# Weight sums at half the pace, one seventh raw buffer, and a quarter of the residual rows scaled earlier: a two-layer fp32 decoder trunk on one core

## The chip, the cores and the metric

One Trainium2 chip, one core in use. The metric is the device time of one execution in microseconds; the times shown are medians over several executions. Engines are named as the profile names them: PE (TensorE matmul), PEld (its weight load), DVE (VectorE), ACT (ScalarE), POOL (GpSimd), SP (SyncE, which here only issues DMAs). Lnnn is line nnn of the kernel before.

## The reference

Two layers, 512 tokens, width 2048, all in fp32. Per layer:

```python
h = einsum('bsd,dn->bsn', x, w_in)             # one projection, split into three head groups
y_fox = fox_attention(q, k, v, cum_logf)       # 6 heads, causal, with a forget bias
y_dsa = dsa_attention(rope(q), rope(k), v, q_idx, k_idx, w_idx)   # 6 heads, top 128 keys by an indexer
y_mem = memory_attention(q, k_mem, v_mem)      # 4 heads over 256 memory tokens
y = concat([y_g * silu(gate_g) for the three groups])
x = layer_norm(ALPHA * x + y @ w_out, ln_gain, ln_bias)
```

## The kernel before

**Matrix products.** TensorE is used in the format fp32r. Each fp32 operand is split into a high and a low part (`split`: ACT copies the high part, L218, DVE subtracts it, L219), and a product is three matmuls (L225 to L227). The weights come in chunks of 128 x 2048 from one long tensor `wall`. A chunk is two halves of 128 x 1024. SP loads a half into one of six `raw` buffers (L259); its split goes to one of four pairs `whi`/`wlo`; PE then uses it.

**Order of the work.** The main loop walks over the chunks in a list written out by hand, and PE runs in that order. Per layer: `mv`, `mk` (memory keys and values, 8 chunks), `small`, `iq` (indexer, 8), `vs` (values, gates and part of the queries, 70), heads (16 chunks `fq`, `fk`, `dq`, `dk`) and `out` (28). While chunk i runs, chunk i+2 is loaded (`load_w`) and the half 1.5 chunks ahead is split. Everything else is a generator that is advanced by `tick`, once in the middle and once at the end of a chunk; a generator that yields k rests for k ticks. Those begun with `whole=True` get no tick in the middle of a `vs` or `out` chunk. The value of `now[1]` names the stage: kv, index, values, heads, out.

**Strassen form.** `vs` and `out` are computed by Winograd's variant of Strassen's product: seven products over five pairs of column blocks (`vs`), each with two chunks (g = 0, 1). The 70 `vs` chunks are numbered here from 0: pair p takes 10p to 10p+9 in the order P1 P1 P7 P7 P2 Q6 Q6 P2 Q4 Q4, then come four chunks for each pair, 50+4p to 53+4p, in the order Q5 Q5 Q3 Q3. The right-hand sides are sums of weight blocks, made in four ways:

- T3 (for P7), and T1 (for Q5) of the pairs below `IN_DRAM`, are made in DRAM by POOL's DMAs, 1 MB each: a copy (L427), then an accumulating DMA (L407). `value_sums` yields after each, `paced` says how many ticks pass to the next, and `load_w` later loads the sum (`raw<-sum`). Outside the stage "values" each such DMA is also held back until DVE has come to a mark (`pool_waits`, L397 and L398).
- T1 of the other pairs is made on chip: SP loads the second block in four pieces into `slots` (`other`, L265) and DVE adds it to the raw halves (`pair_w`, L276).
- Q6 grows out of P7: POOL accumulates one more block from DRAM into the raw half (`grow_w`, L284).
- Q4 comes out of Q6 and P2: DVE adds the two raw halves (`make_w`, L294). Until then P7's four halves and two of P2's are all held.

**Buffers.** Everything else lives in one pool of 71 `slots` of 128 x 512; a new tile takes the slot that was set free longest ago, and its first instruction waits until that slot is really free. DMAs wait in the same way at the head of their queue: SP and POOL each issue strictly in order. Results of `vs` are stored to DRAM (`store_v`, L977 and L979) and loaded again head by head (`load_head`, L986). `attend` handles one head, `mem_head` one memory head (`MEM_TURNS` says after which chunks heads 1 to 3 begin).

**Between the layers.** `next_x` normalises the residual `z`, turns it (PE), applies gain and bias by column on ACT (L1053) for the next projection, makes the low parts on DVE and POOL (L1057), and stores the bare normalised `z` to `x1_d` (L1040). `residual_rows`, in the `vs` stage of layer 1 from chunk 6 on, loads these 16 tiles again (L1087), applies gain and bias by row (L1077, L1078; the rows come from `load_row`, L1027) and stores them (L1079) for the residual of layer 1.

Of the kernel before, what the change touches and what calls it, by code (L numbers as in the profile page):

```python
# [14 lines left out]
ALU = mybir.AluOpType  # L15
# [32 lines left out]
HEADS = (("f", 0), ("f", 4), ("f", 5), ("f", 1), ("d", 0), ("d", 1), ("f", 2), ("d", 2), ("d", 3),  # L48
         ("f", 3), ("d", 4), ("d", 5))
EARLY = 4  # L50
MEM_TURNS = [("fq", 4), ("fk", 4), ("fk", 5)]
HEAD_CHUNKS = ([(c, h) for h in range(EARLY, H_FOX) for c in ("fq", "fk")]
               + [(c, h) for h in range(H_DSA) for c in ("dq", "dk")])

# [27 lines left out]
             ("Q5", 0), ("Q5", 1), ("P2", 0), ("Q3", 0), ("P2", 1), ("Q3", 1))  # L82
PAIRS = 5
MEMQ, FOXQ, VALUES, GATES = 0, 2, 4, 7
IN_DRAM = 2
VAL_FIRST = (("P1", 0), ("P1", 1), ("P7", 0), ("P7", 1), ("P2", 0), ("Q6", 0), ("Q6", 1), ("P2", 1),
             ("Q4", 0), ("Q4", 1))
VAL_SECOND = (("Q5", 0), ("Q5", 1), ("Q3", 0), ("Q3", 1))
# [89 lines left out]
def kernel(  # L178
# [12 lines left out]
):  # L191
    nc = tc.nc
    consts = ctx.enter_context(tc.tile_pool(name="consts", bufs=1))
    raws = ctx.enter_context(tc.tile_pool(name="raws", bufs=6))
    whl = ctx.enter_context(tc.tile_pool(name="whl", bufs=4))
    slots = ctx.enter_context(tc.tile_pool(name="slots", bufs=71))
    tiny = ctx.enter_context(tc.tile_pool(name="tiny", bufs=3))
    psum = ctx.enter_context(tc.tile_pool(name="psum", bufs=8, space=bass.MemoryType.PSUM))
    dram = ctx.enter_context(tc.tile_pool(name="dram", bufs=1, space=bass.MemoryType.DRAM))
# [227 lines left out]
                            nc.gpsimd.dma_start(sums[key], src)  # L427
                        yield

    def paced(gen, steps=2):  # L430

        n = 0
        for _ in gen:
            n += 1
            while now[1] == "kv":
                yield 1
            yield {"heads": 1, "out": 3, "index": 2}.get(now[1], steps)

    def value_sums(l):

# [24 lines left out]
    now = (0, "index")  # L465
# [267 lines left out]
    def attend(l, kind, h):  # L733
        key = (kind, h)
        if kind == "f":
            bt = pr = biases.pop(h)
        q, k = qs.pop(key), ks.pop(key)
        ps = [bank("s") for _ in range(3)]
        for qb in (3, 1, 0, 2):
            b, off, w = PACK[qb]  # L740
            product(ps[b][:, off:off + w], tuple(a[:, qb * P:(qb + 1) * P] for a in q),
                    tuple(a[:, :w] for a in k), True, True)
        if kind == "d":
            assert l in chosen
            bt = masks[l]
            pr = [slot("pr", w=w) for w in BANK_W]
        nm, sums, rec = small("nm", 4), small("sums", 4), small("rec", 4)

        for qb in (3, 1, 0, 2):
            b, off, w = PACK[qb]  # L750
            c = slice(off, off + w)
            nc.vector.tensor_tensor_reduce(pr[b][:, c], ps[b][:, c], bt[b][:, c], -SCALE, -TAKEN,
                                           ALU.add, ALU.min, nm[:, qb:qb + 1])
        for qb in (3, 1, 0, 2):
            b, off, w = PACK[qb]
            nc.scalar.activation(pr[b][:, off:off + w], pr[b][:, off:off + w], AF.Exp,
                                 bias=nm[:, qb:qb + 1], scale=-1.0, accum_out=sums[:, qb:qb + 1])

        def probabilities():
            nc.vector.reciprocal(rec, sums)  # L760
            for qb in (3, 1, 0, 2):
                b, off, w = PACK[qb]
                nc.scalar.activation(pr[b][:, off:off + w], pr[b][:, off:off + w], AF.Copy,
                                     scale=rec[:, qb:qb + 1])

        before.append(probabilities)
        n = HEADS.index(key)
        load_head(("g", key), GATES + n // 4, n % 4)
        load_head(("v", key), VALUES + n // 4, n % 4)
        yield 2  # L770
        tp = [bank("pt") for _ in range(3)]
        for kt in range(4):
            tb, toff = PT_PACK[kt]
            for qb in range(kt, 4):
                b, off, w = PACK[qb]
                nc.tensor.transpose(tp[tb][:, toff + (qb - kt) * P:toff + (qb - kt + 1) * P],  # L776
                                    pr[b][:, off + kt * P:off + (kt + 1) * P], ident)
        pt = []
        for b in range(3):
            w = PT_W[b]  # L780
            if w == 512:
                hi, lo = slot("pth", F32R), slot("ptl", F32R)
            else:
                both = slot("pthl", F32R)
                hi, lo = both[:, :w], both[:, w:]
            split(tp[b][:, :w], hi, lo)
            pt.append((hi, lo))
        yield 1
        gate(key, turned(("g", key), "gt"))
        v = slot("vh", F32R), slot("vl", F32R)  # L790
        split(vraw.pop(("v", key)), *v)
        yield 1
        po = bank("po")
        for kt in range(4):
            tb, toff = PT_PACK[kt]
            w = SEQ - kt * P
            product(po[:, kt * P:], tuple(a[:, kt * P:(kt + 1) * P] for a in v),
                    tuple(a[:, toff:toff + w] for a in pt[tb]), kt == 0, kt == 3)
        heads_out(head_number(key), key, po)
# [182 lines left out]
    def load_head(key, j, c):  # L982

        assert all(stored[j, st] == 1 + j % 2 for st in range(4))
        t = vraw[key] = slot("vraw")
        nc.sync.dma_start(t.rearrange("p (s c) -> p s c", s=4),  # L986
                          v_d[j].rearrange("(s p) c -> p s c", s=4)[:, :, c * HD:(c + 1) * HD])
# [20 lines left out]
    z, stats = {}, {}  # L1008
# [13 lines left out]
    rows = {}  # L1022

    def load_row(l, c, eng):
        for name, src in (("g", gain), ("b", bias)):
            t = rows[name, c] = slot("row")
            eng.dma_start(t, bass.AP(tensor=src.tensor, offset=src.offset + l * DM + c * 512,  # L1027
                                     ap=[[0, P], [1, 512]]))
# [8 lines left out]
    def next_x():  # L1037

        def store(st, c):
            nc.gpsimd.dma_start(x1_d[st * P:(st + 1) * P, c * 512:(c + 1) * 512], z.pop((st, c)))  # L1040

        ms = [norm_stats(st) for st in range(4)]
        for c in range(4):
            for st in range(4):
                normalise(st, c, *ms[st])
            yield 1
        for k in range(KT):
            c, o = divmod(k, 4)
            tp = bank("xt")
            for st in range(4):  # L1050
                nc.tensor.transpose(tp[:, st * P:(st + 1) * P], z[st, c][:, o * P:(o + 1) * P], ident)
            xf, hi, lo = slot("xf"), slot("xh", F32R), slot("xl", F32R)
            nc.scalar.activation(xf, tp, AF.Identity, bias=gcol[:, 1, k:k + 1],  # L1053
                                 scale=gcol[:, 0, k:k + 1])
            nc.scalar.activation(hi, xf, AF.Copy)
            eng = nc.gpsimd if k % 2 else nc.vector
            eng.tensor_tensor(lo, xf, hi.bitcast(F32), op=ALU.subtract)  # L1057
            xT[k] = (hi, lo)
            first_sum(k, xf)
            if k % 2:  # L1060
                for st in (o - 1, o) if c else ():
                    store(st, c - 1)
                yield 1
        for st in range(4):
            store(st, 3)
            if st % 2:
                yield 1

    def residual_rows(l):

        tiles = [(st, c) for c in range(4) for st in range(4)]
        t = {}
        for n in range(len(tiles) + 1):
            if n:
                st, c = tiles[n - 1]
                d = t.pop(n - 1)
                nc.vector.tensor_tensor(d, d, rows["g", c], op=ALU.mult)  # L1077
                nc.vector.tensor_tensor(d, d, rows["b", c], op=ALU.add)  # L1078
                nc.gpsimd.dma_start(x1_d[st * P:(st + 1) * P, c * 512:(c + 1) * 512], d)  # L1079
                if st == 3:  # L1080
                    del rows["g", c], rows["b", c]
            if n < len(tiles):
                st, c = tiles[n]
                if st == 0:
                    load_row(l - 1, c, nc.sync)
                t[n] = slot("z")
                nc.sync.dma_start(t[n], x1_d[st * P:(st + 1) * P, c * 512:(c + 1) * 512])  # L1087
            yield 2

    terms = {}  # L1090

# [68 lines left out]
    for i, (kind, l, j, col, _) in enumerate(chunks):  # L1160
        late = last_half(i)
        if kind == "out":
            step = OUT_ORDER.index(j)
            name, pair = j
# [11 lines left out]
        elif kind == "vs":  # L1176
            name, pair = j
# [11 lines left out]
        for h in range(2):  # L1189
            n = 2 * i + h  # L1190
# [15 lines left out]
            if kind == "out" and late:  # L1206
# [6 lines left out]
                if len(kept) == 16:  # L1213
# [3 lines left out]
                    for c in (0, 256):  # L1217
                        ps = bank("z")
                        c = slice(c, c + 256)
# [17 lines left out]
            elif kind == "mv":  # L1237
                for m in range(2):
                    for nn in range(2):
                        k = 4 * col + 2 * h + nn  # L1240
                        c = (k % 2) * 256 + m * P
# [3 lines left out]
            elif kind == "mk":  # L1245
                for kk in range(8):
                    k = 8 * h + kk
                    m = memT[k // 2]
                    c = (k % 2) * 256
                    product(ps[:, :256], weight_cols(n, kk), tuple(a[:, c:c + 256] for a in m),  # L1250
                            k == 0, k == KT - 1)
            else:
                cols = slice(P if kind == "iq" else 0, SEQ)
                for kk in range(8):
                    k = 8 * h + kk
# [9 lines left out]
        if kind == "mk":  # L1265
            t = slot("kmem", F32R)
# [14 lines left out]
        elif kind in ("dq", "dk"):  # L1281
            t = rope(ps, cos_d, sin_d, HALVES, P, "rope")
# [8 lines left out]
        elif kind == "small":  # L1291
# [4 lines left out]
            t = index_rope(ps, 64, 0, nc.vector)  # L1296
            kh2, kl2 = slot("kh2", F32R), slot("kl2", F32R)
            for r in (0, 64):
                nc.scalar.activation(kh2[r:r + 64], t[:64], AF.Copy)
                nc.vector.tensor_tensor(kl2[r:r + 64], t[:64], kh2.bitcast(F32)[:64],  # L1300
                                        op=ALU.subtract)
            idx["k"] = (kh2, kl2)
            begin(small_work(l, sm))
        elif kind == "iq":
            t = index_rope(ps, P, P, nc.gpsimd)
# [12 lines left out]
        if kind == "mv" and l > 0:  # L1318
            now = (l, "kv")
        if kind == "small":  # L1320
            now = (l, "index")
# [140 lines left out]
```

## Time and profile before

| | |
|---|---|
| median of 3 runs | 1934.21 us (1932.75 to 1935.8) |
| the profiled execution | 1935.36 us, span 1933.6 us |
| granted TensorE clock | 0.994 |
| PE busy | 1898.5 us, 98% of the span |
| DVE, ACT, POOL busy | 1469.4, 1016.7, 372.9 us |
| DMA moved | 503.55 MB, mean 260 GB/s |

The profile is read in this way: PE is busy nearly always, so what can be won without changing the arithmetic are the stretches in which it waits or runs at a lower clock. Matmul durations overlap one another, so the count of matmuls in a stretch says more than the busy time.

### The profile page before, as it was taken

What the parts mean: (1) busy time and instruction counts of PE and PEld (TensorE: products, weight loads), DVE (VectorE), ACT (ScalarE), POOL (GpSimd) and SP (SyncE); (2) the same over time, 40 slices, a digit from 0 to 9 for tenths busy, and PEclk for the clock granted to TensorE, in tenths of its full rate; (3) what the DMA queues carried; (4) which work ended last, traced back from release to release, by engine and by line L of the source; (5) the groups of instructions that cost most, each with busy time, mean ns of one, the idle gap of its engine ahead of it and who ended that gap; (6) DMA issues with size and microseconds to landing.
All of it is one profiled execution on the core that took longest, in us unless ns stands there. A gap on an engine that the chain in (4) does not pass through costs nothing.

```text
span 1933.6 us, 26367 instructions
## 1 busy us (share of the span) xinstructions
PE 1898.5 (98%) x9250; PEld 1612.4 (83%) x9250; DVE 1469.4 (76%) x2374; ACT 1016.7 (53%) x1598; POOL 372.9 (19%) x610
## 2 busy tenths in 40 slices
PE   9999999999999999999999999999999999999997
PEld 8998777888888888888899987778888888888886
DVE  6888667887755677688877886799877566677888
ACT  5676334355456555554476753444544465555453
POOL 0122221221222012110061221221113120112101
PEclk9999999999999999999999999999999999999999
DMA  9777988999988788999886799987899786889966
GB/s 353 260 204 205 292 251 287 252 271 279 343 262 223 222 263 237 259 331 293 262 269 225 202 244 312 273 281 236 236 287 352 254 240 193 265 241 260 348 198 152
DMA packets 169906, 503.55 MB, mean 260 GB/s; under 512 B 17120, under 2 KB 62176, under 8 KB 160876
## 3 DMA queue, kind: packets, MB, share of 16 engines
q1 hardware_dynamic: 132876, 296.28, 44.5%
q0 software_dynamic: 36896, 205.57, 41.4%
q8 instruction: 73, 1.20, 0.2%
q14 instruction: 61, 0.50, 0.1%
HBM read 453.53 MB, written 176.19 MB: 326 GB/s over the span
## 4 chain that ended last, share of the span: by engine, by line
PE 70%; DMA 11%; DVE 11%; ACT 4%; issue 2%; POOL 1%; SPq 0%; DVEq 0%; ACTq 0%; POOLq 0%
DMA raw<-in_wall_dram 10%; PE v L226 8%; PE v L227 8%; PE v L225 8%; PE c L227 8%; PE c L225 8%; PE c L226 8%; DVE wlo L219 4%; PE z L226 4%; PE z L227 4%; PE z L225 4%; ACT whi L218 2%; PE pt L776 1%; DVE raw L294 1%; PE ix L693 1%
## 5 line engine op out<-in xcount | busy, mean ns | idle before, releaser
L219 DVE TENSOR_TENSOR wlo<-raw,whi 128x1024 fp32r<-128x1024 f32 (+1 forms) x521 | 634.7, 1224 | 273.6 <-ACT whi L218 270.2
L218 ACT ACTIVATE whi<-raw 128x1024 fp32r<-128x1024 f32 (+1 forms) x521 | 547.1, 1054 | 457.3 <-PE v L227 179.3
L225 PE MATMUL c<-xh,whi 128*128 128x512 f32 (+1 forms) x800 | 301.3, 377 | 0.0
L227 PE MATMUL c<-xh,wlo 128*128 128x512 f32 (+1 forms) x800 | 298.4, 373 | 0.0
L226 PE MATMUL c<-xl,whi 128*128 128x512 f32 (+1 forms) x800 | 297.8, 372 | 0.0
L226 PE MATMUL v<-wlo,vxh 128*128 128x512 f32 x640 | 249.5, 390 | 2.4 <-DVE wlo L219 2.4
L225 PE MATMUL v<-whi,vxh 128*128 128x512 f32 x640 | 249.7, 390 | 0.2 <-ACT whi L218 0.2
L227 PE MATMUL v<-whi,vxl 128*128 128x512 f32 x640 | 249.1, 389 | 0.0
L226 PE MATMUL v<-wlo,xh 128*128 128x512 f32 x480 | 190.2, 396 | 8.4 <-DVE wlo L219 8.4
L225 PE MATMUL v<-whi,xh 128*128 128x512 f32 x480 | 189.6, 395 | 6.0 <-ACT whi L218 5.9
L227 PE MATMUL v<-whi,xl 128*128 128x512 f32 x480 | 189.1, 394 | 0.0
L226 PE MATMUL z<-wlo,yh 128*128 128x512 f32 (+1 forms) x434 | 168.1, 387 | 2.5 <-DVE wlo L219 2.5
L225 PE MATMUL z<-whi,yh 128*128 128x512 f32 (+1 forms) x434 | 168.4, 388 | 0.0
L227 PEld LDWEIGHTS c<-xh,wlo 128*128 128x128 f32 x800 | 150.1, 188 | 21.9
L227 PE MATMUL z<-whi,yl 128*128 128x512 f32 (+1 forms) x434 | 167.8, 387 | 0.0
L226 PEld LDWEIGHTS c<-xl,whi 128*128 128x128 f32 x800 | 150.4, 188 | 20.7
L225 PEld LDWEIGHTS c<-xh,whi 128*128 128x128 f32 x800 | 150.3, 188 | 20.3
L226 PEld LDWEIGHTS v<-wlo,vxh 128*128 128x128 f32 x640 | 120.1, 188 | 28.6 <-DVE wlo L219 3.8
L398 POOL TENSOR_TENSOR seen<-mark,mhalf 128x1 f32<-128x1 f32 x91 | 23.6, 259 | 620.3 <-DVE mark L397 611.6
L225 PEld LDWEIGHTS v<-whi,vxh 128*128 128x128 f32 x640 | 120.1, 188 | 25.6 <-ACT whi L218 0.9
L227 PEld LDWEIGHTS v<-whi,vxl 128*128 128x128 f32 x640 | 120.1, 188 | 25.1
L226 PEld LDWEIGHTS v<-wlo,xh 128*128 128x128 f32 x480 | 91.3, 190 | 31.9 <-DVE wlo L219 12.9
(227 smaller groups left out, 3215.7 us busy)
## 6 DMA issues: line engine op xcount, KB each, us to landing
raw<-in_wall_dram SPq DMA_DIRECT2D x322, 512.0 KB, 7.4
sum<-in_wall_dram POOLq DMA_DIRECT2D x60, 1024.0 KB, 11.6
raw<-sum SPq DMA_DIRECT2D x120, 512.0 KB, 7.6
v<-vraw POOLq DMA_DIRECT2D x120, 256.0 KB, 7.2
raw<-in_wall_dram POOLq DMA_DIRECT2D x48, 512.0 KB, 9.4
vraw<-v SPq DMA_DIRECT2D x80, 256.0 KB, 6.7
other<-in_wall_dram SPq DMA_DIRECT2D x48, 256.0 KB, 8.8
x<-z POOLq DMA_DIRECT2D x32, 256.0 KB, 6.7
```

The lines of the kernel that those rows point to most:

```text
L218: nc.scalar.activation(hi, src, AF.Copy)
L219: nc.vector.tensor_tensor(lo, src, hi.bitcast(F32), op=ALU.subtract)
L225: nc.tensor.matmul(ps, ah, bh, start=start, stop=False, skip_group_check=more)
L226: nc.tensor.matmul(ps, ah, bl, start=False, stop=False, skip_group_check=more)
L227: nc.tensor.matmul(ps, al, bh, start=False, stop=stop, skip_group_check=more)
L294: nc.vector.tensor_tensor(t, t, raw[lender][h], op=ALU.add)
L398: nc.gpsimd.tensor_tensor(seen, mark, mhalf, op=ALU.mult)
L693: nc.tensor.matmul(o, st[:, qb * P:(qb + 1) * P], kh2[:, :w], start=True, stop=False)
L776: nc.tensor.transpose(tp[tb][:, toff + (qb - kt) * P:toff + (qb - kt + 1) * P], pr[b][:, off + kt * P:off + (kt + 1) * P], ident)
```

## The change

The sums of the `vs` stage are issued every 4 ticks (every 2 before) in the stage "values", and in the stage "index" after 2 and 1 ticks by turns (2 before). T1 is made in DRAM for pair 0 only, and on chip for pairs 1 to 4. There are seven raw halves (six before) and 69 slots (71 before), which is the same space. `mem_head` 2 begins after chunk `fq` 5 (before: after `fk` 4). `attend` loads its values one tick after its gates, not together with them. `next_x` loads the gain and bias rows of the last column block by SP and scales its four tiles itself before it stores them, one per tick; `residual_rows` handles the other 12 tiles, one every 3 ticks (before: 16, one every 2).

```diff
-MEM_TURNS = [("fq", 4), ("fk", 4), ("fk", 5)]
+MEM_TURNS = [("fq", 4), ("fq", 5), ("fk", 5)]
...
-IN_DRAM = 2
+IN_DRAM = 1
...
-    raws = ctx.enter_context(tc.tile_pool(name="raws", bufs=6))
+    raws = ctx.enter_context(tc.tile_pool(name="raws", bufs=7))
...
-    slots = ctx.enter_context(tc.tile_pool(name="slots", bufs=71))
+    slots = ctx.enter_context(tc.tile_pool(name="slots", bufs=69))
...
-    def paced(gen, steps=2):
+    def paced(gen, steps=4):
...
-            yield {"heads": 1, "out": 3, "index": 2}.get(now[1], steps)
+            yield {"heads": 1, "out": 3, "index": 1 + n % 2}.get(now[1], steps)
...
         load_head(("g", key), GATES + n // 4, n % 4)
+        yield 1
         load_head(("v", key), VALUES + n // 4, n % 4)
-        yield 2
+        yield 1
...
                 for st in (o - 1, o) if c else ():
                     store(st, c - 1)
+                if k == 13:
+                    load_row(0, 3, nc.sync)
                 yield 1
         for st in range(4):
+            scale_row(z[st, 3], 3)
             store(st, 3)
-            if st % 2:
-                yield 1
+            yield 1
+        del rows["g", 3], rows["b", 3]
+
+    def scale_row(t, c):
+        nc.vector.tensor_tensor(t, t, rows["g", c], op=ALU.mult)
+        nc.vector.tensor_tensor(t, t, rows["b", c], op=ALU.add)
...
-        tiles = [(st, c) for c in range(4) for st in range(4)]
+        tiles = [(st, c) for c in range(3) for st in range(4)]
...
-            yield 2
+            yield 3
```

More of the change, by code (lines that the diff above doesn't have):

```diff
@@ L1076, in residual_rows @@
                 d = t.pop(n - 1)
-                nc.vector.tensor_tensor(d, d, rows["g", c], op=ALU.mult)
-                nc.vector.tensor_tensor(d, d, rows["b", c], op=ALU.add)
+                scale_row(d, c)
                 nc.gpsimd.dma_start(x1_d[st * P:(st + 1) * P, c * 512:(c + 1) * 512], d)
```

## The prediction

> **What bounds the kernel now.** First the page, to see which engine sets the end.
>
> ```profile
> span 1933.6 us, 26367 instructions
> PE 1898.5 (98%) x9250; PEld 1612.4 (83%) x9250; DVE 1469.4 (76%) x2374; ACT 1016.7 (53%) x1598; POOL 372.9 (19%) x610
> PE 70%; DMA 11%; DVE 11%; ACT 4%; issue 2%; POOL 1%; SPq 0%; DVEq 0%; ACTq 0%; POOLq 0%
> ```
>
> PE idles for only 35 us, yet a tenth of the chain is DMA. So I asked in which stage PE falls behind, by windows restricted to the matmuls that write `v` (start:end, length, PE busy with its count, ... clock, DMA share, GB/s).
>
> ```profile
> 172.60:381.20 208.60, 201.12 (x866) 162.44 (x865) 9.29 (x14) 11.92 (x21) 17.72 (x30) 0.99 0.91 264
> 381.20:533.40 152.20, 152.20 (x673) 126.05 (x672) 3.92 (x6) 13.39 (x23) 19.43 (x27) 1.00 0.98 301
> 1131.10:1342.90 211.80, 202.31 (x866) 164.33 (x865) 9.61 (x15) 12.15 (x21) 16.62 (x30) 0.98 0.89 272
> 1342.90:1495.10 152.20, 152.20 (x673) 126.05 (x672) 3.61 (x6) 13.64 (x23) 19.45 (x27) 1.00 0.97 292
> ```
>
> A `vs` chunk is 24 of these matmuls, so the second row is chunks 40 to 67 of layer 0 at full pace: 152.2 / 672 = 0.2265 us a matmul, 5.44 us a chunk. The first row is chunks 4 to 39: 36 x 5.44 = 195.8 us of work in 208.6, 12.8 us lost. The third is the same in layer 1: 16.0 us lost. Together 28.8 us, and none in the second halves. That is the pot; the rest of the kernel holds few idle microseconds that this change touches.
>
> What is late there: the waits of PE in the two stretches, of ACT and SP in the first (us in total, times, longest), then the landing times of DMAs for 200:340 (the first two, in the bad stretch) and for 381:440 (the last two, in the good one).
>
> ```profile
> PE v L226 <- DVE wlo L219: 5.0, 8, 0.8
> PE v L225 <- ACT whi L218: 2.3, 2, 1.5
> PE v L226 <- DVE wlo L219: 5.8, 6, 2.3
> PE v L225 <- ACT whi L218: 3.7, 2, 3.6
> ACT whi L218 <- DMA raw<-in_wall_dram: 54.4, 18, 6.9
> SPq L259 <- DVE raw L294: 134.5, 16, 25.2
> raw<-in_wall_dram SPq DMA_DIRECT2D x18, 512.0 KB, 8.5
> raw<-sum SPq DMA_DIRECT2D x10, 512.0 KB, 15.6
> raw<-in_wall_dram SPq DMA_DIRECT2D x8, 512.0 KB, 7.5
> raw<-sum SPq DMA_DIRECT2D x6, 512.0 KB, 4.9
> ```
>
> PE waits for splits, splits for raw halves, and a half loaded from a sum takes 15.6 us to land in the bad stretch against 4.9 in the good one. SP also loses 134.5 us until `make_w` gives buffers back, so it issues late and in bunches. What else moves are the sums (tile `sum`, 147.6:400, then 1106:1350 for layer 1).
>
> ```profile
> L407 POOL DMA_DIRECT2D sum<-in_wall_dram x12: 829/1180/1475, 151.5 to 371.6; - x12
> L427 POOL DMA_DIRECT2D sum<-in_wall_dram x8: 507/834/856, 165.1 to 317.8; - x8
> DMA to landing us min/median/max: 8.1/13.5/26.6
> L407 POOL DMA_DIRECT2D sum<-in_wall_dram x7: 817/916/1177, 1110.0 to 1226.3; - x7
> ```
>
> The last sum of layer 0 is issued at 371.6, and the losses end by 381.2; in layer 1 the sums end at 1226.3 and the losses fade out in the next 60 us. So I read the sums as the main cause and the ring of six raw halves as what makes PE feel it.
>
> **The change part by part, costed.**
>
> *Fewer and slower sums.* I counted ticks through the list of chunks. Layer 0 before: 9 of 28 sums by the end of `iq`, then one per two chunks to chunk 37 (the trace's 371.6). After: 24 sums, 11 by the end of `iq`, one at chunk 0, then 12 at chunks 4, 8 ... 48. Layer 1 before: ten, at chunks 1 to 19; after three, at 1, 5 and 9, since the index stage takes more of them. A sum that needs 13.5 us came every 10.9 us; now it comes every 21.8, so DMA has gaps. Loss per sum in layer 0: 19 of them (chunks 1 to 37) cost 12.8 us, 0.67 each. Nine remain before chunk 40, so 6.0 us if they cost as much each, nothing if the spacing frees them. I take 2.0, nearer the free end, since without sums but still with residual traffic nothing was lost (second row below). Layer 1: by count 16.0 x 3 / 10 = 4.8 us, at best nothing; I take 1.5, as the last stall there is DVE's (first row: 46.22 us busy of 54.4).
>
> ```profile
> 1240.00:1294.40 54.40, 50.52 (x212) 40.14 (x211) 46.22 (x68) 23.36 (x26) 8.20 (x14) 0.97 0.87 272
> 1294.40:1342.90 48.50, 48.50 (x216) 40.16 (x215) 44.65 (x63) 22.09 (x24) 9.49 (x15) 1.00 0.76 237
> L1077 DVE TENSOR_TENSOR z<-z,row x16: 679/682/685, 1161.6 to 1338.9; 128x512 f32<-128x512 f32 x16
> L1078 DVE TENSOR_TENSOR z<-z,row x16: 691/692/694, 1162.3 to 1339.6; 128x512 f32<-128x512 f32 x16
> ```
>
> *Residual rows.* A tile costs DVE 0.682 + 0.692 = 1.37 us and a load and a store of 256 KB. Every third chunk instead of every second frees 0.23 us of DVE a chunk (5.44 us) and a third of that traffic, to chunk 45 instead of 40. Four tiles (5.5 us of DVE, four loads) leave the stage. It is within the 1.5 above.
>
> *Seventh half.* SP may fetch one half (2.72 us of PE) earlier. It shortens the 134.5 us; it is why I take the low ends. It costs two slots.
>
> *T1 of pair 1 on chip.* Four sums go per layer; eight pieces of 256 KB and eight DVE adds come, near chunks 52 to 54.
>
> ```profile
> L276 DVE TENSOR_TENSOR raw<-raw,other x48: 680/684/694, 469.3 to 1484.4; 128x512 f32<-128x512 f32 x48
> 446.00:457.00 11.00, 11.00 (x50) 9.13 (x49) 5.68 (x6) 5.33 (x6) 1.77 (x2) 1.00 0.89 241
> 457.00:468.00 11.00, 11.00 (x51) 9.09 (x50) 7.74 (x12) 5.33 (x6) 1.79 (x3) 1.00 0.94 272
> 468.00:479.00 11.00, 11.00 (x50) 9.13 (x49) 10.93 (x18) 5.34 (x6) 1.83 (x3) 1.00 1.06 359
> 425.72 1.07 POOL L979 DMA_DIRECT2D v<-vraw  x2 [3.15 <-ACT vraw L952]
> ```
>
> 8 x 0.684 = 5.5 us on a DVE that works 13.4 of 22 us there: 18.9 of 22, which the next pair already does (third of the windows: 10.93 of 11) without PE losing anything. Zero, covered by that slack; without it 5.5 a layer.
>
> *The last sum is late: a new wait.* The second chunk of Q5 for pair 0 is chunk 51, which starts at 381.2 + 11 x 5.44 = 441.0. Its sum is now issued at the end of chunk 48's turn, on POOL behind the two stores of P2, which wait for ACT (last row: 425.72 + 1.07), so at 426.8. It lands 8.1 to 13.5 us later; I take 9.5, near the low end because SP stands still then and queues nothing. SP, blocked in order with Q3's loads behind it, then needs 4.9 for the half, 1.06 for ACT and 1.22 for DVE (estimates from the rows of their kind: 547.1 us over 521 and 634.7 over 521 on the page), and PE asks at 441.2: 426.8 + 9.5 + 7.2 + 0.5 of issue and hand-over - 441.2 = 2.8 us (1.4 to 5.8). Layer 1's last sum is issued 41 chunks ahead: nothing.
>
> Would such a stall slow the clock too?
>
> ```profile
> 304.00:308.00 4.00, 2.40 (x8) 1.38 (x7) 2.10 (x2) 3.03 (x4) 0.00 (x0) 0.93 0.06 25
> 308.00:312.00 4.00, 4.00 (x13) 3.21 (x12) 3.97 (x7) 1.35 (x3) 0.00 (x0) 0.64 0.42 131
> ```
>
> Here 1.6 us of idling in 4 was followed by a granted clock of 0.64: 0.36 x 4 = 1.4 us lost. [...] Elsewhere such waits left the clock at 1.00, so I keep 2.8 and put 1.4 into the upper end.
>
> *The layer boundary (`next_x`).* Two slots fewer, two row loads on SP, eight DVE operations more (waits and timeline 985:1010, then landing times of row loads over the whole run, by SP and by POOL).
>
> ```profile
> ACT xf L1053 <- DMA x<-z: 3.6, 1, 3.6
> PE c L227 <- DVE wlo L219: 0.5, 1, 0.5
> 1004.61 1.49 DVE L219 TENSOR_TENSOR wlo<-raw,whi 128x1024 fp32r<-128x1024 f32 x1 [1.52 <-ACT whi L218]
> row<-in_bias_dram SPq DMA_DIRECT2D x4, 256.0 KB, 25.7
> row<-in_bias_dram POOLq DMA_DIRECT2D x4, 256.0 KB, 5.9
> ```
>
> ACT already waits 3.6 us for slots that a store of `z` sets free, and PE hangs right behind the splits (0.5 us for the low part of 1004.61). With 69 slots ACT waits for a later store, about 1.7 us more; four times 1.37 us of scaling go between splits that PE needs every 2.9 us, which just fits. SP's row loads need slots too, so the weight loads behind them go out later. If rows land only after 25.7 us, DVE stands in front of them and PE loses some 11 us; if after 5.9 us, nothing. I take 3.0 (0.5 to 11): the weights around 990 to 1000 land within 10 us.
>
> *Heads.* SP waits long for slots there (540:840), and two slots fewer lengthen that; `MEM_TURNS` and the split loads shorten it.
>
> ```profile
> SPq L986 <- PE po L227: 55.8, 7, 13.2
> SPq L986 <- PE pt L776: 38.2, 3, 20.5
> ACT whi L218 <- DMA raw<-in_wall_dram: 0.5, 1, 0.5
> ```
>
> Weights are late for ACT by 0.5 us in all, and PE has up to three split halves (3 x 5.4 us) in hand. Zero, covered by those 16 us; uncovered, whatever SP's waits grow beyond them.
>
> **Sum.** -12.8 + 2.0 - 16.0 + 1.5 + 2.8 + 3.0 = -19.5 us. The profiled execution took 1935.4 us (span 1933.6), 1.2 above the median of 1934.2, so 1915.9 for it and 1914.7 as a median: 1915.
>
> **Rivals.**
>
> *A. The ring and DVE, not the sums.* For it: SP's 134.5 us; the last loss in layer 1 comes after its sums, at 46.22 of 54.4 us of DVE. Against it: chunks 40 to 49 run at full pace with nearly the same ring. Half of the 28.8 stays: 1934.2 - 14.4 + 5.8 = 1925.6.
>
> *B. Slower.* The heads run out of slots: SP stands in order, weights land late. It decides where a wait of SP grows by more than the 16 us that PE holds. To undo the gain it must cost over 19.5 + 3.9 us, 12 per layer, so a wait of 20 must become 48: 1915 + 2 x 13 = 1941. Against it: the 0.5 above.
>
> *C. Nothing moves.* The sums only shift into chunks 40 to 48 and the stalls with them: 1934 +- 3.9. Against it: the DMA share is 0.91 with losses and 0.98 without, so more room is there than the share tells.
>
> *D. Boundary.* Rows and slots at their upper end: 1914.7 - 3 + 11 = 1923.
>
> **Chances.** Forecast (1906 to 1921) 0.60, A and D (1921 to 1930) 0.24, C 0.07, B 0.09. About 0.2%, 3.9 us, is what a measurement of this kernel can tell from no change. Faster 0.84, same 0.07, slower 0.09. Range: lowest with only the low ends of the two new waits, 1934.2 - 28.8 + 1.4 + 0.5 = 1907.3, set to 1906; the upper ends together give 1934.2 - 28.8 + 6.0 + 4.8 + 7.2 + 11 = 1934; to leave 2 in 10 out, A and D are taken in to 1928. The forecast's own range is 1908 to 1921.
>
> **What would show it.** In the profile after: chunks 4 to 39 within 3 us of 195.8 in each layer; `raw<-sum` landing in under 10 us; PE waiting a few us near chunk 51 of layer 0; ACT's wait for `x<-z` above 3.6; heads unchanged. It is wrong if PE still waits for splits while no sum is in flight, or if SP's waits in the heads reach ACT.

## The result, and the profile after

The changed kernel takes 1921.27 us in the median of four runs (1920.23 to 1925.35), the kernel before 1933.48 in the runs beside it (1931.9 to 1935.8): a ratio of 0.994, 95% interval 0.9922 to 0.9958, or 12.2 us less. The prediction said 1915, with 1906 to 1928 as its range: the time lies inside it, but 12.2 us were gained where some 19 were forecast. The profiled execution after took 1921.65 us.

From the page of the changed kernel: the span, the busy times, and the chain that ended last.

```profile
span 1919.9 us, 26427 instructions
PE 1891.7 (99%) x9250; PEld 1611.7 (84%) x9250; DVE 1482.1 (77%) x2395; ACT 1019.6 (53%) x1598; POOL 364.5 (19%) x603
PE 82%; DVE 7%; ACT 5%; DMA 3%; issue 2%; POOL 0%; SPq 0%; DVEq 0%; ACTq 0%; POOLq 0%
```

DMA fell from 11% of the chain to 3%, as it should if loads were what PE waited for. The windows of the matmuls that write `v` show where: chunks 4 to 39 of layer 0, chunks 40 to 67, then the same of layer 1.

```profile
172.90:368.70 195.80, 195.80 (x865) 162.22 (x864) 9.59 (x15) 12.59 (x21) 16.52 (x30) 1.00 0.83 242
368.70:528.30 159.60, 156.02 (x674) 128.17 (x673) 3.65 (x6) 13.51 (x23) 19.49 (x27) 0.98 0.99 303
1129.80:1325.60 195.80, 195.80 (x866) 162.18 (x865) 9.60 (x15) 12.60 (x21) 16.27 (x30) 1.00 0.79 238
1325.60:1477.90 152.30, 152.30 (x673) 126.16 (x672) 3.63 (x6) 13.63 (x23) 19.56 (x27) 1.00 1.00 307
```

Rows one and three now last 195.8 us with PE busy in all of it: the whole pot of 12.8 and 16.0 us is gone. Row two has a new loss: 159.6 us for what took 152.2. What lies behind the first row, in the order of the waits of ACT and SP in that stretch, the landing of halves loaded from sums in 200:340, and the sums of layer 0 themselves (tile `sum`, 140:440):

```profile
ACT whi L218 <- PE v L227: 88.2, 56, 1.7
SPq L259 <- DVE raw L294: 129.2, 16, 21.7
raw<-sum SPq DMA_DIRECT2D x9, 512.0 KB, 6.1
L407 POOL DMA_DIRECT2D sum<-in_wall_dram x9: 815/922/1195, 141.3 to 414.3; - x9
```

ACT no longer waits for data but for PE, that is, for a free buffer: the splits run ahead. A half from a sum lands in 6.1 us instead of 15.6. SP still stands 129.2 us (134.5 before) for `make_w`'s buffers, so that wait was not what made PE late.

**The late last sum.** POOL's timeline (start, duration), the tile `sum` in 410:432 (loads of halves, the sum, landing min/median/max), SP's wait in 400:440, ACT's first split, PE's waits in 420:450, and windows (the clock stands third from the end).

```profile
413.27 1.07 POOL L980 DMA_DIRECT2D v<-vraw  x2 [3.15 <-ACT vraw L953]
414.33 0.92 POOL L407 DMA_DIRECT2D sum<-in_wall_dram  x1
L259 SPq DMA_DIRECT2D raw<-sum x2: 319/346/372, 425.4 to 425.8; - x2
DMA to landing us min/median/max: 3.9/4.7/11.0
SPq L259 <- DMA sum<-in_wall_dram: 39.1, 2, 22.3
429.41 1.06 ACT L218 ACTIVATE whi<-raw 128x1024 fp32r<-128x1024 f32 x1 [8.92 <-DMA raw<-sum]
PE v L225 <- ACT whi L218: 1.8, 1, 1.8
PE v L225 <- ACT vraw L968: 1.0, 1, 1.0
PE v L226 <- DVE wlo L219: 0.8, 1, 0.8
428.00:430.00 2.00, 0.71 (x4) 0.25 (x2) 0.00 (x0) 0.59 (x1) 0.00 (x0) 1.00 0.95 383
430.00:431.00 1.00, 0.48 (x1) 0.19 (x1) 0.50 (x1) 0.80 (x2) 0.00 (x0) 1.00 1.02 320
431.00:437.80 6.80, 6.04 (x15) 4.82 (x15) 6.70 (x12) 3.25 (x4) 1.10 (x2) 0.50 1.00 396
```

The sum leaves POOL behind the stores and lands 11.0 us later, at 425.3; the half lands 3.9 us after its issue, ACT splits at 429.41, and PE, which wanted chunk 51 at 428.5, waits. Then the clock stays at 0.50 for 6.8 us, which costs 3.4 us. Chunks 50 and 51 together take 18.0 us for 10.9: 7.1 lost, 3.6 in waits and the rest in the clock.

**The heads and the boundary.** PE's waits in the heads of layer 0 (636:660) and of layer 1 (1585:1610), then PE's and ACT's at the layer boundary (975:1040 and 975:1015).

```profile
PE c L225 <- DVE rope L580: 1.5, 1, 1.5
PE po L227 <- DVE vl L219: 0.5, 1, 0.5
PE po L225 <- ACT vh L218: 0.2, 1, 0.2
PE c L225 <- DVE rope L580: 1.4, 1, 1.4
PE po L227 <- DVE vl L219: 0.5, 1, 0.5
PE ix L693 <- DVE iqs L679: 2.6, 1, 2.6
PE c L227 <- DVE wlo L219: 0.3, 1, 0.3
ACT xf L1054 <- DMA x<-z: 3.2, 1, 3.2
```

In both heads stages PE waits for DVE and ACT, for `rope` and for the split values, not for weights; the kernel before has no wait there. By the starts of the same chunks in the two traces, the new order is first 1.8 and 1.9 us ahead at `dq` 0, since 16 short matmuls, 12 of them memory scores (`sm`), now come later, and then falls back by 4.6 and 4.7 up to `dk` 1: 2.9 and 2.8 us lost, of which 2.2 and 1.9 are the waits shown. In chunk `dq` 1 of layer 0 DVE now works 15.5 of 21.7 us and ACT 11.8 (before: 11.2 of 17.2, and 8.3), while in `dk` 0, the chunk ahead of it, DVE works 9.4 us (13.6 before). Adding up the starts after minus before: -12.4 (chunk 40 of layer 0), +7.1 (chunks 50 and 51), +2.9 (heads), +1.1 (boundary), -16.0 (layer 1 to chunk 40), +2.8 (heads), +0.8 (out): -13.7, the difference of the spans.

### The profile page after: what moved, and what is told of

Read it like the earlier page. It is cut to its first block, busy times and chain, and to the rows that moved or that the text cites. A ratio compares the mean times of both kernels' runs of the same rounds, so it can differ in the third digit from the quotient of the medians.

```text
span 1919.9 us, 26427 instructions
## 1 busy us (share of the span) xinstructions
PE 1891.7 (99%) x9250; PEld 1611.7 (84%) x9250; DVE 1482.1 (77%) x2395; ACT 1019.6 (53%) x1598; POOL 364.5 (19%) x603
## 4 chain that ended last, share of the span: by engine, by line
PE 82%; DVE 7%; ACT 5%; DMA 3%; issue 2%; POOL 0%; SPq 0%; DVEq 0%; ACTq 0%; POOLq 0%
PE v L227 13%; PE v L225 13%; PE v L226 13%; PE c L225 7%; PE c L227 7%; PE c L226 7%; PE z L226 4%; PE z L227 4%; PE z L225 4%; DVE wlo L219 2%; ACT whi L218 2%; DMA raw<-sum 1%; DMA raw<-in_wall_dram 1%; PE ix L693 1%; PE pt L777 1%
## 6 DMA issues: line engine op xcount, KB each, us to landing
sum<-in_wall_dram POOLq DMA_DIRECT2D x56, 1024.0 KB, 10.9
```

## The experiments

The kernel before had medians of 1933.5, 1937.2, 1937.2, 1934.0 and 1934.9 us in the five sets of runs, so a ratio belongs to its own set, and places are read from the profiles.

**1. Sums every third tick.** On the changed kernel:

```diff
-    def paced(gen, steps=4):
+    def paced(gen, steps=3):
```

> The changed kernel with one sum every 3 ticks in the values stage instead of every 4, so that layer 0's last sum is issued at chunk 36 and not at 48. Theory (the 7.2 us that the changed kernel loses at chunks 50 and 51 of layer 0 are the lateness of the last sum): that loss goes and nothing comes back, 1921.3 - 7.2 = 1914 us. Rival (the pace of 4 is what clears the first forty chunks): 13 sums between chunks 3 and 39 instead of nine jam the loads again, by 13/19 of the 12.8 us lost before, and the kernel stays at 1921 to 1923 us. A third reading (the stall is slow landing and not late issue): the loss at chunk 51 stays as it is, 1921 us.

1913.97 us, ratio 0.9886 (0.9866 to 0.9905), span 1911.9. The last sum now leaves at 330.3 instead of 414.3; the loss at chunks 50 and 51 is gone whole, and chunks 4 to 39 keep full pace. The heads lose as before (4.5 us between `dq` 1 and `dk` 1 in layer 0). A pace of 4 was slower than needed.

**2. Order of the memory heads undone.** On the changed kernel:

```diff
-MEM_TURNS = [("fq", 4), ("fq", 5), ("fk", 5)]
+MEM_TURNS = [("fq", 4), ("fk", 4), ("fk", 5)]
```

> The changed kernel with memory head 2 begun after fk 4 again. Theory (memory heads 2 and 3, now two ticks apart, bunch work of DVE and ACT, so that the rope of dq1 comes late and PE waits for its PSUM bank): the 2.8 us that each layer loses between dq1 and dk1 go, 1921.3 - 5.7 = 1915.6 us. Rival (values loaded one tick later in attend): nothing changes, 1921 us, and the next run shows it. Rival (two slots fewer): 1921 us or slower, as the earlier memory head asks for more slots at once; SP's longest waits in the heads grow.

1915.93 us, ratio 0.9896 (0.9877 to 0.9915), span 1914.9. PE has no wait in either heads stage, and both losses there are gone; the one at chunk 51 stays (here 9.0 us with chunk 52). So the order of the memory heads alone costs the 5.7 us.

**3. Split loads of `attend` undone.** On the changed kernel:

```diff
         load_head(("g", key), GATES + n // 4, n % 4)
-        yield 1
         load_head(("v", key), VALUES + n // 4, n % 4)
-        yield 1
+        yield 2
```

> The changed kernel with gates and values of a head loaded together again. Theory (memory heads bunch): no change, 1921 us, the 2.8 us a layer near dq1 stay. Rival (the values' low part vl comes late since its load is issued a tick later, PE waits 0.86 us for it and what follows is late too): the loss near dq1 goes, 1915.6 us.

1919.97 us, ratio 0.9917 (0.9902 to 0.9933), which overlaps the changed kernel's. The losses in the heads stay as they were: this edit is worth nothing that shows.

**4. The sums of the change alone.** On the kernel before, with six halves and 71 slots:

```diff
-IN_DRAM = 2
+IN_DRAM = 1
-    def paced(gen, steps=2):
+    def paced(gen, steps=4):
-            yield {"heads": 1, "out": 3, "index": 2}.get(now[1], steps)
+            yield {"heads": 1, "out": 3, "index": 1 + n % 2}.get(now[1], steps)
```

> The kernel before with the sums of the changed kernel alone (T1 in DRAM for pair 0, pace of 4, 2 and 1 by turns in the index stage); six raw halves, 71 slots, residual rows as before. Theory (the sums are the main cause): of the 28.8 us lost in chunks 4 to 39 at most 6 stay, and the late last sum costs about 7: 1933.5 - 22.8 + 7 = 1918 us. Rival (the ring of six halves and a full DVE set the losses): half stays, 1933.5 - 14.4 + 7 = 1926 us.

1915.24 us, ratio 0.9892 (0.9873 to 0.9911), span 1913.4. Both stretches run at full pace, chunks 50 to 52 lose 8.2 us, heads and boundary nothing. The sums alone do all that the whole change does in chunks 4 to 39; the other edits added nothing there and cost 5.7 in the heads.

**5. Everything but the sums.** On the changed kernel, the edit of experiment 4 the other way round (`IN_DRAM` 2, 2 ticks everywhere):

> The changed kernel with the sums as before: T1 in DRAM for pairs 0 and 1, every 2 ticks, also in the index stage. Kept: the seventh half, 69 slots, the residual rows in two places, the order of the memory heads, the split loads of attend. Theory (sums alone cause the loss of chunks 4 to 39, the order of the memory heads costs 5.7 us): 1933.5 + 5.7 = 1939, a little less (1935 to 1939) if the seventh half and the residual rows take some of the jam, and PE still waiting for splits in chunks 4 to 39. Rival (the ring was the cause, either remedy is enough): the stalls go here too, 1939.2 - 28.4 = 1911, or 1925 if half of them go.

1920.67 us, ratio 0.9919 (0.9901 to 0.9936). My theory fell: most of the loss goes without touching the sums. These are the matmuls of `v` in chunks 4 to 39 of this run, layer 0 and layer 1:

```profile
173.30:370.80 197.50, 196.45 (x866) 162.11 (x865) 9.62 (x15) 12.19 (x21) 16.98 (x30) 1.00 0.97 284
1123.60:1323.70 200.10, 197.30 (x865) 162.03 (x865) 9.58 (x15) 12.43 (x21) 16.68 (x30) 1.00 0.91 274
```

With the old sums, 1.7 and 4.3 us are lost instead of 12.8 and 16.0. Rival A of the prediction, the ring, was refuted as the only cause by experiment 4; but here one or more of the other edits takes most of the loss by itself, and the ring is among them. So I split the question: pace, number of sums, ring, residual rows, each alone on the kernel before.

**6. Pace alone.** Still 28 sums per layer:

```diff
-    def paced(gen, steps=2):
+    def paced(gen, steps=3):
-            yield {"heads": 1, "out": 3, "index": 2}.get(now[1], steps)
+            yield {"heads": 1, "out": 3, "index": 1 + n % 2}.get(now[1], steps)
```

> The kernel before with the pace alone: sums every 3 ticks, 2 and 1 by turns in the index stage, still 28 sums a layer (T1 of pairs 0 and 1 in DRAM). Layer 0 then has 16 sums from chunk 3 to chunk 48, 16.3 us apart; layer 1 seven from chunk 1 to chunk 19. Theory (a threshold: a sum takes about 13.5 us to land, so sums 10.9 us apart overlap and sums 16.3 us apart don't): full pace in both layers, 1905 to 1908. Rival (the number of sums costs, 0.67 us each, as my prediction had it): layer 0 keeps 13 of its 19 sums before chunk 40 and layer 1 seven of ten, so 8.8 and 11.2 us of loss stay: about 1925.

1909.67 us, ratio 0.986 (0.9842 to 0.9878).

```profile
173.40:369.20 195.80, 195.80 (x866) 162.18 (x865) 9.60 (x15) 12.58 (x21) 16.55 (x30) 1.00 0.85 256
1119.10:1317.30 198.20, 196.37 (x865) 162.08 (x864) 9.56 (x15) 12.18 (x21) 16.20 (x30) 1.00 0.87 269
```

Layer 0 loses nothing, though 13 sums still run in it before chunk 40, where the price of 0.67 us per sum would leave 8.8; layer 1 keeps 2.4 of 16.0, and the time lies above the 1905 to 1908 that the theory gave. In layer 0, then, the number of sums is not what costs.

How the pace works is seen in POOL's queue. First the kernel before: rows of POOL's timeline (start, duration, idle time before; rows in between are left out), and the landing times of the three sums of 336:343. For this run the sums of 314:332 follow.

```profile
313.68 0.58 POOL L979 DMA_DIRECT2D v<-vraw  x1 [25.64 <-DVE vraw L956]
316.26 0.51 POOL L427 DMA_DIRECT2D sum<-in_wall_dram  x1
317.85 0.51 POOL L427 DMA_DIRECT2D sum<-in_wall_dram  x1
338.27 1.18 POOL L407 DMA_DIRECT2D sum<-in_wall_dram  x1
338.84 1.51 POOL L284 DMA_DIRECT2D raw<-in_wall_dram  x1
341.64 2.02 POOL L407 DMA_DIRECT2D sum<-in_wall_dram  x2
DMA to landing us min/median/max: 12.4/21.6/26.6
```

This run, sums and landing times:

```profile
L427 POOL DMA_DIRECT2D sum<-in_wall_dram x3: 509/818/841, 316.6 to 330.0; - x3
DMA to landing us min/median/max: 8.5/10.9/12.4
```

The sums don't come every 10.9 us, because POOL issues in order. It stands up to 25.6 us before a store of `v`, and behind the stores two sums go within 2 us. Then it stands before the accumulations of `grow_w` (L284, 512 KB each), which wait for splits, and among these go three sums within 4 to 7 us; the last of the three shown takes 26.6 us to land. This happens three times between chunks 4 and 39 of layer 0 of the kernel before (219.6 to 226.2, 280.4 to 287.2, 338.3 to 342.2), and by the starts of the chunks 9.0 of its 12.8 us are lost behind them, in chunks 13 and 14, 26 to 28, and 38. At a pace of 3 at most two sums of this stretch stand so close, and nothing is lost.

Layer 1 needs no threes. The seven sums of the kernel before from 1155.4 to 1226.3 stand 5.4 to 21.2 us apart, no three of them within 7 us, and 16.0 us are lost; in this run five sums, 11.1 to 25.2 us apart, leave 2.4; in experiment 7 three sums, 8.4 and 14.5 us apart, leave 9.3. So sums that stand closer go with more loss there as well, and the stores of the residual rows (L1079), which are issued by POOL too, come on top (experiment 9). That the pace is a cause is shown; that it works through the groups is argued, as no run changed the groups without the pace.

**7. Number alone.** `IN_DRAM = 1`, still every 2 ticks:

> The kernel before with T1 in DRAM for pair 0 only and nothing else: 24 sums a layer, still every 2 ticks, the last at chunk 29 of layer 0 (37 before) and chunk 11 of layer 1 (19 before); six halves. Theory (spacing, not number): layer 0 loses the same through chunk 30, so 11 to 12 of 12.8 stay; in layer 1 the sums end eight chunks earlier, and what follows them (8 to 14 of 16.0) goes: 1933.5 - 1 - 11 = 1921, range 1917 to 1927. Rival (each sum costs its share): 4 of 19 in layer 0 and 4 of 10 in layer 1, -2.7 - 6.4 = 1924.4, with the losses thinned evenly over the chunks, not cut off at the end. The two differ more in the place than in the time.

1927.96 us, ratio 0.9964 (0.9952 to 0.9977). Neither time was met; both were too low. The place speaks for spacing: layer 0 loses as much as before (209.4 - 195.8 = 13.6) while dense sums run; in layer 1, where the last sum leaves in chunk 12, all 9.3 us are lost by the end of chunk 14 and none after, where the kernel before lost until chunk 29.

**8. Ring alone.** On the kernel before:

```diff
-    raws = ctx.enter_context(tc.tile_pool(name="raws", bufs=6))
+    raws = ctx.enter_context(tc.tile_pool(name="raws", bufs=7))
-    slots = ctx.enter_context(tc.tile_pool(name="slots", bufs=71))
+    slots = ctx.enter_context(tc.tile_pool(name="slots", bufs=69))
```

> The kernel before with seven raw halves and 69 slots, nothing else. The run with the old sums lost only 2.0 us in chunks 4 to 39 of layer 0, where no residual rows are handled, so there the ring must have taken the other 10.8. Theory (ring and spacing are two remedies of one jam, each nearly enough alone): layer 0 -11, layer 1 -8 to -12 as well, heads and boundary unchanged: 1933.5 - 21 = 1912, range 1910 to 1917. Rival (in layer 1 it was the slower residual rows): layer 1 keeps its 16.0, 1923. Second rival (69 slots cost something in the heads): 2 us or more lost between dq 0 and the out stage.

1916.31 us, ratio 0.9906 (0.989 to 0.9922). The two stretches; PE's waits in the first; landing times in 200:340; then the boundary: ACT's wait, and two windows.

```profile
172.90:370.50 197.60, 196.44 (x865) 161.82 (x864) 9.56 (x15) 12.16 (x21) 17.19 (x30) 1.00 0.96 282
1122.90:1323.80 200.90, 197.39 (x866) 161.79 (x865) 9.59 (x15) 12.43 (x21) 16.65 (x30) 1.00 0.92 287
PE v L226 <- DVE wlo L219: 1.0, 1, 1.0
sum<-in_wall_dram POOLq DMA_DIRECT2D x7, 1024.0 KB, 18.7
raw<-sum SPq DMA_DIRECT2D x9, 512.0 KB, 12.6
ACT xf L1053 <- DMA x<-z: 5.4, 1, 5.4
992.00:996.00 4.00, 2.82 (x13) 2.62 (x14) 2.25 (x3) 3.88 (x8) 2.65 (x4) 0.74 0.87 336
996.00:1000.00 4.00, 4.00 (x31) 4.00 (x30) 4.00 (x5) 3.30 (x5) 3.39 (x7) 0.83 0.66 234
```

The sums still land late (18.7 us for the copies), halves from them take 12.6 us, the DMA share is 0.96, and PE loses only 1.8 us in layer 0, 5.1 in layer 1. The stretch of layer 0, with the same sums in it, now runs at 282 GB/s (264 before), so the mean load is not more than the DMA engines can carry. One more half in hand covers most of the lateness. But the boundary loses 3.2 us up to the start of `mk` 3: ACT's wait grew from 3.6 to 5.4, PE waited 1.5 us for splits, and the clock was 0.74 and 0.83 in the two windows of 4 us, which costs 1.7.

**9. Residual rows alone.** The edits in `next_x` and `residual_rows`, on the kernel before with 71 slots:

> The kernel before with the residual rows alone as in the change: next_x scales four of 16 tiles, residual_rows takes one tile every 3 ticks; six halves, 71 slots, old sums. Theory (little DVE work and traffic leaves the jam): layer 0 unchanged, layer 1's 16.0 falls by 0 to 4, the boundary costs 0 to 1: 1930 to 1934. Rival (the residual traffic and DVE's 1.37 us per tile are what makes layer 1 worse than layer 0): -8 or more, 1925 or less. If the price of 3.0 for the boundary was right, PE loses it between the last out chunk and iq 2.

1928.73 us, ratio 0.997 (0.9959 to 0.9982). In layer 1:

```profile
1131.70:1335.80 204.10, 198.89 (x866) 161.50 (x865) 9.61 (x15) 12.19 (x21) 16.68 (x30) 1.00 0.88 266
```

8.3 lost instead of 16.0, so 7.7 went: the rival (8 or more) was nearer than the theory (0 to 4), though the time lies between the two. Layer 0 keeps its loss (13.4). Whether DVE's time or the traffic did it was not separated.

**10. Sums alone, every third tick** (experiment 4 with `steps=3`), and **11. the changed kernel with both faults mended** (`steps=3`, `MEM_TURNS` as before):

> The kernel before with three edits: T1 in DRAM for pair 0 only, sums every 3 ticks in the values stage, 2 and 1 ticks by turns in the index stage; six raw halves, 71 slots and all else as before. Theory (the sums are the whole cause, and the last one only has to be early enough): chunks 4 to 39 at full pace in both layers (-12.4 and -16.0), no loss at chunks 50 and 51, heads and boundary as before: 1933.5 - 28.4 = 1905, with 1903 to 1908 as its range; the run with every fourth tick minus its loss at chunk 51 gives nearly the same, 1915.2 - 8.4 = 1906.8. Rival (at 16.3 us between sums a ring of six halves jams again, and only the seventh made the pace of 3 harmless): some of the 28.4 comes back, 1912 or more, with PE waits on splits in chunks 4 to 36 of layer 0.

> The changed kernel with sums every 3 ticks and memory head 2 begun after chunk fk 4 again. Theory (the two losses are independent): 1914.0 - 5.3 = 1908.7, range 1907 to 1911, no wait near chunk 51 and none of the 2.8 us between dq 1 and dk 1 in either layer. Rival (heads and sums share the DMA queues, so one gain eats the other): 1911.5 or more. Against the kernel before with the sums alone it tells what the seventh half, the 69 slots, the residual rows and the split loads of attend are worth together: nothing within 2 us is expected.

1907.04 us (1906.4 to 1907.3), ratio 0.9845 (0.9828 to 0.9863), and 1906.97 (1906.48 to 1909.38), ratio 0.9848 (0.983 to 0.9866). Both beat both kernels, the changed one by 15 us (spans of 1905.1 and 1904.7 against 1919.9), and equal each other: once the sums are paced right, the other edits together buy nothing that shows. These are the stretches of the second:

```profile
172.60:368.40 195.80, 195.80 (x865) 162.17 (x864) 9.55 (x15) 12.58 (x21) 16.60 (x30) 1.00 0.88 257
1118.20:1314.00 195.80, 195.80 (x865) 162.25 (x864) 9.55 (x15) 12.59 (x21) 16.27 (x30) 1.00 0.79 237
```

**12. Sums every third tick and the ring**, with `next_x` and `residual_rows` as before:

> The kernel before with the sums as in the best version (pair 0 only, every 3 ticks, 2 and 1 by turns in the index stage) and seven halves with 69 slots; next_x and residual_rows as before. It asks what the residual rows of the change are good for. Theory (69 slots alone cost the boundary 3.2 us, as in the run with the ring alone, where ACT's wait for x<-z grew from 3.6 to 5.4 and PE hung behind the splits; scaling in next_x takes that back): 1907 + 3.2 = 1910, all of it between the last out chunk of layer 0 and the index chunks of layer 1, with PE waiting for whi or wlo of c. Rival (the 3.2 was one disturbed execution): 1907, boundary within 0.6 of before.

1908.86 us (1908.67 to 1909.01), ratio 0.9864 (0.9848 to 0.9881). ACT's and PE's waits at the boundary, and two windows:

```profile
ACT xf L1053 <- DMA x<-z: 5.2, 1, 5.2
PE c L227 <- DVE wlo L219: 1.6, 2, 1.0
988.00:992.00 4.00, 2.73 (x20) 2.33 (x20) 2.41 (x3) 3.88 (x6) 2.31 (x3) 1.00 0.95 348
992.00:996.00 4.00, 3.43 (x28) 3.23 (x28) 2.40 (x4) 3.97 (x7) 2.94 (x5) 1.00 0.62 220
```

The median lies between theory and rival, and its interval overlaps that of experiment 10, so the place decides. The wait of over 5 us is there again; in experiment 10, with 71 slots and six halves, it is 3.3. So it goes with the ring and its 69 slots, and up to `iq` 2 it costs 1.8 us here, without a fall of the clock. In the change it is 3.2, and in experiment 9, with 71 slots and the new `next_x`, it is gone: the edits of `next_x` and `residual_rows` take back what the two slots cost. How they do it was not tested.

Losses of chunks 4 to 39, from the lengths of such windows less 195.8 us:

| kernel | layer 0 | layer 1 |
|---|---|---|
| before | 12.8 | 16.0 |
| fewer sums alone (7) | 13.6 | 9.3 |
| residual rows alone (9) | 13.4 | 8.3 |
| ring alone (8) | 1.8 | 5.1 |
| all but the sums (5) | 1.7 | 4.3 |
| pace alone (6) | 0.0 | 2.4 |
| sums of the change (4, 10), the change, 11 | 0.0 to 0.1 | 0.0 |

## Why the prediction was right, and where its steps were wrong

*The pot.* Right: 28.8 us in chunks 4 to 39, all of it for this change to take.

*The remainders, 2.0 and 1.5.* Measured 0.0 each. The price of 0.67 us per sum had the wrong form, and "every 10.9 us" was read from the code: POOL issues the sums in groups (experiment 6). Layer 0 loses nothing once they stand further apart, where a price per sum leaves a share; in layer 1 five sums behind chunk 4 at a pace of 3 still leave 2.4 (experiment 6), and a single one leaves nothing (experiment 10). How sums and residual rows share the blame there stays open. The low ends I took were right; the reason I gave, the seventh half, was not needed.

*Seventh half and residual rows.* I put both inside other terms. Alone, the half takes 21.9 us of the 28.8, and the rows take 7.7 in layer 1. With the 28.8 of the sums that is twice the pot: they are remedies of one jam, and once the sums are spaced the others add nothing. The two slots that the half takes were priced at the boundary together with the scaling; without the new `next_x` and `residual_rows` they go with a loss of 3.2 and 1.8 there (experiments 8 and 12; the clock is 1.7 of the 3.2).

*The boundary, +3.0.* No sum stood behind the 3.0. It was 1.1 in this execution, in a wait of `ix` for `iqs` (2.6 us, before 1.3) that is 1.3 again in experiments 1 to 3, with the same code at the boundary, and no loss in experiment 11. The predicted sign, ACT's wait above 3.6, was wrong: 3.2.

*T1 on chip, 0.* Right: no loss at chunks 50 to 60 wherever the last sum was early (experiments 1, 10, 11).

*The late last sum, +2.8.* The mechanism was right to a few tenths in time: predicted issue 426.8, less the 12.4 gained before it 414.4, measured 414.33. Its size was not: the sum took 11.0 us to land, not 9.5, the half 3.9, not 4.9, PE waited 3.6 us in all instead of 2.8, and the clock added 3.4 that I had kept out of the sum. The 7.1 us lie just below the upper end that the prediction had for this term, 5.8 and 1.4 for the clock. The lower price rested on waits elsewhere that had left the clock at 1.00. In the kernel before that holds for 1.49 and 0.77 us of waiting between 230.6 and 233.3, but not for a wait of 3.57 us that ended at 1206.5, nor for one of 2.31 us that ended at 1278.8 (last section). Here the longest wait was 1.80 us, and the clock was at 0.50 for 6.8 us. The row of the trace (304 to 312) pointed the right way, and its lesson was the one to put into the sum; its price was 1.7 us, not 1.4, as the clock fell at 307.4 already (the 0.93 of the row above).

*The heads, 0.* The step that failed outright. I named as cover the halves of weights in hand, and asked of `MEM_TURNS` only whether weights come late. They do not; PE waits for `rope` and the split values, work of DVE and ACT that bunches in chunk `dq` 1 now that two memory heads start two ticks apart. 5.7 us, shown by experiment 2. Undone, nothing is lost.

With these measures the sum is -19.5 + 4.3 (last sum) + 5.7 (heads) - 3.5 (remainders) - 1.9 (boundary) + 0.8 (out) = -14.1, against the -13.7 of the spans. The time came near because two misses stood on one side and smaller ones on the other, and that is luck: 1921.27 lies just above the 1908 to 1921 of the forecast itself, in the band that the prediction kept for the rivals A and D, and neither of them is what happened.

*Rivals.* C and B fell: nothing is lost in chunks 40 to 49, the one stall comes at chunk 51, and in the heads ACT never waits for a weight load. D gave nearly the right number by the wrong cause. A was half right, as experiment 8 shows: one more half alone takes most of the loss.

## What to carry to other kernels

Look at when a queue really issues its transfers, not at the pace in the code: POOL's queue, which issues in order, released the sums here in groups of two and three, and what they cost went with their spacing (in layer 0 12.8 us at 2 ticks, nothing at 3) and was no price for each. Spacing, a deeper ring and less other traffic were substitutes here, whose gains did not add. Spacing has an end of its own: work out when the last transfer is due at its consumer, since a pace of 4 lost 7.1 us that a pace of 3 did not. And for a step that is moved, name the cover for each of its operands (here values and rotated heads from DVE and ACT), not for the weights alone.

## What the runs showed of the hardware

**The clock.** Without the first and the last 20 us, the traces of the kernel before and of the changed kernel have four stretches at a granted clock of 0.50, and 1.00 everywhere else. The waits of PE are those just ahead of each stretch; the one of 3.57 us ends within it.

| kernel | at 0.50 from | for | PE waited | until |
|---|---|---|---|---|
| before | 307.4 | 3.4 us | 0.84 and 0.76 us | 305.9 and 307.2 |
| before | 1205.1 | 6.8 us | 3.57 us | 1206.5 |
| before | 1280.2 | 3.4 us | 2.31 us | 1278.8 |
| changed | 431.0 | 6.8 us | 1.80 us | 430.5 |

Other waits left the clock at 1.00: 1.49 and 0.77 us up to 232.1 and 233.3 in the kernel before, and in the changed kernel 2.60 us up to 1039.9 (`ix` for `iqs`) and 1.45 us up to 658.1 and up to 1607.8. In experiment 8 waits of 1.0 and 0.5 us went with a clock of 0.74 and 0.83 in the two windows of 4 us, in experiment 12 waits of 1.6 and 0.3 us with 1.00 in both. So the length of a wait did not tell whether the clock would fall, as 2.60 us left it at 1.00 and 1.80 us were followed by 0.50; what decides was not shown.

A DMA share of 0.97 and 0.96 went with losses of only 1.7 and 1.8 us (chunks 4 to 39 of layer 0, experiments 5 and 8), and 0.91 and 0.89 with losses of 12.8 and 16.0 us (the two layers of the kernel before): the share of busy time did not tell which kernel was short of data.
